# Transposed projection blocks in halves of 256 columns, with the high and low parts of x^T as one moving operand of 512

## The chip, the cores and the metric

The kernel runs on one core of a Trainium2 chip. Times are device microseconds of one launch. TensorE multiplies (a matmul streams the columns of its moving operand past a stationary one of up to 128x128, loaded before), VectorE (DVE), ScalarE (ACT) and GpSimd (POOL) do the elementwise work, SyncE (SP) issues most transfers. Matmul results land in PSUM, in banks of 512 fp32 columns per partition.

## What is computed

Two layers of a decoder trunk for 256 tokens of width 2048. Each layer normalises x, projects it once, runs four groups of four heads in parallel, gates each and projects back onto the residual:

```python
h = rms_norm(x, norm_g)
p = split_columns(h @ w_in)            # 2048 x 7700
fox  = forgetting_attention(...) * silu(p["fox_g"])
diff = rms_norm(differential_attention(...)) * silu(p["diff_g"])
moba = moba_attention(...) * silu(p["moba_g"])   # rotary on a part of q and k
gla  = rms_norm(gla_chunked(...)) * silu(p["gla_g"])
x = x + concat([fox, diff, moba, gla]) @ w_out   # 2048 x 2048
```

After both layers comes one more RMS norm. Everything is fp32, so the kernel computes each large product in three parts: an operand is split into a high part (rounded to fp32r, TensorE's fast fp32 form) and a low part (the rest), and a·b becomes ah·bh + ah·bl + al·bh.

## The kernel before, in words

**Blocks and steps.** `_blocks` (L103) lists the projections of a layer in order as blocks of up to 512 columns of weights. A "rows" block makes a result with tokens on the partitions: x^T is stationary, the weights move (n up to 512 columns), for two halves of 128 tokens. A "cols" block makes the transposed result, with weight columns on the partitions: 128 weight columns are stationary and x^T moves, 256 tokens. Nine blocks of a layer are "cols": GLA's q and k together, FoX's q, k and gate, the q and k of the differential attention, and MoBA's q, k and gate. The contraction has 16 tiles of 128 (kt). `_steps` (L138) cuts a block into steps that each take 512 KB of weights: two kt of 512 columns or four of up to 264. The first two blocks of layer 0 (GLA's low-rank input with a part of its gate, 264 columns, four steps; GLA's q and k, eight steps) are interleaved by groups of four kt, since x^T arrives in four chunks: one row step, two column steps, four times.

**The main loop** (L1296) runs over the steps. Each turn first emits `prepare(i + 2)`: the high part of the weights of the step after next on ScalarE (`hi_of`), the low part on VectorE (`lo_of`, source minus high), and the load of a later step on SP's queue. In the first twelve steps, one turn in three also splits a chunk of x^T (`split_xt`): four high and four low pieces of 256 columns. There are three buffers for the split weights, so ScalarE's split waits until TensorE has finished the step before the current one. Then `settle` evacuates finished blocks out of PSUM if the row statistics they need are ready, `multiply` emits the step's matmuls, and `tick` lets each pending task (attention and GLA are written as generators) advance by one part. Emission order is each engine's execution order.

**The planner.** `Costed` (L171) adds up what VectorE and ScalarE were given, at 0.06 us + 1.05 ns and 0.22 us + 0.88 ns per element (L232). `give_time` (L1259) credits both with TensorE's columns / 2400 us, 2.56 us a step, up to 3 us ahead. `tick` stops when an engine is past its credit. Before a step whose input is not ready, tasks are forced without limit.

**PSUM.** The pool `mm` has two buffers of two banks, one per block in turn; `side` has two more for the tasks. A "cols" block fills 4 x 256 columns: four weight groups, each [128, 256].

**The row statistics** of layer 0 come from x^T itself (`first_rms`, L1164): ScalarE squares each chunk in place, VectorE adds chunks 1 and 2 to the first and folds (two adds each for the first and the last), TensorE sums over partitions, POOL takes the power, TensorE spreads the result (`spread_rms`, L439). Until they are there no block is evacuated, as the scale is applied on the way out: `columns` (L457) multiplies a "cols" result by the spread scale, `rotated` (L881) also shuffles partitions for the rotary part, `gla_qk` (L542) scales q and k.

The matmuls of a "cols" step (L1246) are 24: for two kt and four weight groups c

```python
o, cs = ps[:, c * SEQ:(c + 1) * SEQ], slice(c * P, (c + 1) * P)
matmul(o, hi[:, cs], lh[:, kt], first and c % 2 == 0, False)
matmul(o, hi[:, cs], ll[:, kt], False, False)
matmul(o, lo[:, cs], lh[:, kt], False, last and c % 2 == 1)
```

with `lh` and `ll` the high and low parts of x^T. All operations on VectorE and ScalarE go through `Costed` and show line 183, matmuls line 279, transposes line 283; groups are told apart by their tiles.

Of the kernel before, what the change touches and what calls it, by code (L numbers as in the profile page):

```python
# [13 lines left out]
F32 = mybir.dt.float32  # L14
F32R = mybir.dt.float32r
# [86 lines left out]

def _blocks():  # L103

    def block(w, l, c0, n, kind, groups=(0, 1, 2, 3)):
        kts = [g * 4 + i for g in groups for i in range(4)]
        return {"w": w, "l": l, "c0": c0, "n": n, "kind": kind, "kts": kts, "per": 4 if n * 4 <= STEP_W else 2}

    out = []
    for l in range(DEPTH):  # L110
        for kind, c0, n in (
            ("rows", COL["gla_a"], 264),
            ("cols", COL["gla_q"], 512),
            ("rows", COL["gla_g"] + 248, 264),
            ("rows", COL["gla_v"], 512),
            ("rows", COL["fox_v"] + 258, 258),
            ("cols", COL["fox_q"], 512),
            ("cols", COL["fox_k"], 512),
            ("rows", COL["fox_v"], 258),
            ("cols", COL["fox_g"], 512),  # L120
            ("cols", COL["diff_q"], 512),
            ("cols", COL["diff_k"], 512),
            ("rows", COL["diff_g"], 512),
            ("rows", COL["diff_v"], 512),
            ("cols", COL["moba_q"], 512),
            ("cols", COL["moba_k"], 512),
            ("cols", COL["moba_g"], 512),
            ("rows", COL["moba_v"], 512),
        ):
            out.append(block("w_in", l, c0, n, kind))  # L130
        for chunk in range(4):
            cut = l + 1 == DEPTH and chunk == 3
            out.append(block("w_out", l, chunk * 512, 256 if cut else 512, "rows", (3, 0, 1, 2)))
    out.append(block("w_out", DEPTH - 1, D - 256, 256, "apart", (3, 0, 1, 2)))
    return out

# [76 lines left out]
def hybrid_trunk(  # L213
# [114 lines left out]

    def constants():

        nc.scalar.dma_start(ct, const[:, :KEPT])
        yield from until(("h", 0, 3))
        nc.scalar.dma_start(wa[0:16], gla_wa2.rearrange("l r e -> r l e"))
        nc.scalar.dma_start(wa[16:17].rearrange("p l e -> p (l e)"), gla_ba.rearrange("(o l) e -> o (l e)", o=1))
        yield
        s = []
        for name in ("sets", "upto", "masks"):
            c, n = CAT[name]
            s.append(s4.get([P, n], BF16))
            nc.scalar.dma_start(s[-1], const_b[:, c:c + n])  # L340
        yield
        c, n = CAT["neg"]
        nc.scalar.dma_start(neg_b, const_b[:, c:c + n])
        nc.scalar.dma_start(gng.rearrange("p l d -> p (l d)"), bcast_rows(gla_norm_g, 0, DEPTH * HD))
        nc.scalar.dma_start(fb.rearrange("p l h -> p (l h)"), bcast_rows(fox_fb, 0, DEPTH * H))
        yield
        lamt = s2.get([P, DEPTH, 4, 64])
        nc.scalar.dma_start(lamt.rearrange("p l a d -> p (l a d)"), bcast_rows(diff_lam, 0, DEPTH * 256))
        nc.scalar.dma_start(dng.rearrange("p l d -> p (l d)"), bcast_rows(diff_norm_g, 0, DEPTH * HD))
        yield  # L350
        v_.tensor_copy(a_r, s[0])
        v_.tensor_copy(upto_r, s[1])
        v_.tensor_copy(masks.rearrange("p l t -> p (l t)"), s[2])
        v_.tensor_scalar(ones_r, ident, 0.0, 1.0, op0=OP.mult, op1=OP.add)
        s4.put(*s)
        ready.add("constants")
        yield
        lp = s2.get([P, DEPTH, 2, 64])
        for l in range(DEPTH):
            v_.tensor_mul(lp[:, l], lamt[:, l, 0:4:2], lamt[:, l, 1:4:2])  # L360
            v_.tensor_reduce(ls2[:, l], lp[:, l], axis=AX.X, op=OP.add)
        s2.put(lp, lamt)
        yield
        a_.activation(ls2, ls2, AF.Exp)
        yield
        for l in range(DEPTH):
            li = 0.8 - 0.6 * math.exp(-0.3 * l)
            v_.scalar_tensor_tensor(lam[:, l:l + 1], ls2[:, l, 0:1], li, ls2[:, l, 1:2], op0=OP.add, op1=OP.subtract)
            v_.tensor_scalar(dng[:, l], dng[:, l], 1.0 - li, None, op0=OP.mult)

    hT = [big.tile([P, KT, SEQ], F32R, name="hTh"), big.tile([P, KT, SEQ], F32R, name="hTl")]
    mT = [big.tile([P, KT, SEQ], F32R, name="mTh"), big.tile([P, KT, SEQ], F32R, name="mTl")]


# [79 lines left out]
    def over(rb, n):  # L454
        return rb[:, None, :].to_broadcast([P, n, SEQ])

    def columns(l, ps, store):  # L457

        store = store.get([P, H, SEQ])
        v_.tensor_mul(store, ps, over(env["rb", l], H))  # L460
        return store

    def rows_of(l, ps, dst, eng):
        r = env["r", l]
# [74 lines left out]
            a_.activation(sg[:, m, :248], ps[m][:, 16:], AF.Silu, scale=r[:, m:m + 1])  # L539
        tasks.append(gla(l, an))  # L540

    def gla_qk(l, pqk):  # L542
        rb = env["rb", l]
        qkT = s4.get([P, 4, SEQ])
        v_.scalar_tensor_tensor(qkT[:, 0:2], pqk[:, 0:2], 0.125, over(rb, 2), op0=OP.mult, op1=OP.mult)
        v_.tensor_mul(qkT[:, 2:4], pqk[:, 2:4], over(rb, 2))
        env["gla_qk", l] = qkT
        ready.add(("gla_qk", l))

    def gla_gate(l, ps):  # L550
        r, sg = env["r", l], env["gla_sg", l]
# [224 lines left out]
        yield from split_group(l, gi, mixed, lambda: s4.put(mixed))  # L776

    def gate_columns(name):
        def done(l, ps):
            sgT = columns(l, ps, sgs)  # L780
            env[name, l] = sgT

            def silu():
                yield
                a_.activation(sgT, sgT, AF.Silu)
                ready.add((name, l))

            tasks.append(silu())

        return done  # L790
# [61 lines left out]
            yield  # L852
        ready.add(("forget", l))

    def fox_q(l, ps):
        env["fox_q", l] = columns(l, ps, s4)

    def fox_k(l, ps):
        kT = columns(l, ps, s4)

        def run():
            yield from until(("forget", l))
            yield
            yield from attend_columns(l, 0, "fox", env["fox_q", l], kT, env["forget", l])

        tasks.append(run())
# [14 lines left out]
    def rotated(name, table, half, last):  # L881
        swap = [i ^ half if i < 2 * half else i for i in range(32)]

        def done(l, ps):
            f = env[table, l]
            t = s4.get([P, H, SEQ])
            sw = s4.get([P, H, SEQ])
            v_.stream_shuffle(sw, ps, swap)
            v_.tensor_mul(t, ps, over(f[:, 0], H))

            def run():
                yield
                g_.tensor_mul(sw, sw, over(f[:, 1], H))
                yield
                yield
                v_.tensor_add(t, t, sw)
                s4.put(sw)
                if last:
                    s2.put(f)
                env[name, l] = t  # L900
                ready.add((name, l))

            tasks.append(run())

        return done

    def preceded(task, done):

        def both(l, ps):
            done(l, ps)  # L910
            tasks.append(task(l))

        return both

# [116 lines left out]
        yield from attend_columns(l, 2, "moba", env["moba_q", l], env["moba_k", l])  # L1031

    def started(task, done):
        def both(l, ps):
            tasks.append(task(l))
            done(l, ps)

        return both

# [55 lines left out]
    for l in range(DEPTH):  # L1095
# [10 lines left out]
            residual(0), residual(1), residual(2), residual(3),  # L1106
        )]
    dones.append((DEPTH - 1, None))
    blocks = []
    for z, (l, f) in zip(_BLOCKS, dones, strict=True):  # L1110
        own = {COL["diff_q"]: ("rope_d",), COL["moba_q"]: ("rope_m",)}.get(z["c0"] if z["w"] == "w_in" else None, ())
        blocks.append({"kind": z["kind"], "lhs": hT if z["w"] == "w_in" else mT, "n": z["n"], "per": z["per"],
                       "done": f and partial(f, l), "keys": {("r", l), ("rb", l)} | {(k, l) for k in own},
                       "need": "h" if z["w"] == "w_in" else "m", "l": l})
    plan = []
    for z in _steps():
# [11 lines left out]

    def load(i):
        s = plan[i]  # L1130
        if i < 12 and i % 3 == 0:
            load_x(i // 3)
        per, n = s["block"]["per"], s["block"]["n"]
        raw = wst.tile([P, STEP_W], F32, name="raw", bufs=RAW_BUFS)
        raw = raw[:, :per * n]
# [72 lines left out]
    def multiply(s):  # L1208
# [28 lines left out]
        for j, kt in enumerate(s["kts"]):  # L1237
# [6 lines left out]
                    matmul(o, lh[:, kt, ts], lo, False, False)  # L1244
                    matmul(o, ll[:, kt, ts], hi, False, last)
            else:  # L1246
                for c in range(4):
                    o, cs = ps[:, c * SEQ:(c + 1) * SEQ], slice(c * P, (c + 1) * P)
                    matmul(o, hi[:, cs], lh[:, kt], first and c % 2 == 0, False)
                    matmul(o, hi[:, cs], ll[:, kt], False, False)  # L1250
                    matmul(o, lo[:, cs], lh[:, kt], False, last and c % 2 == 1)

    def results(b):
        ps, n = b["ps"], b["n"]
        if b["kind"] == "rows":
            return ps[:, 0:n], ps[:, 512:512 + n]
        return ps.rearrange("p (c t) -> p c t", c=4)

    def give_time():  # L1259

# [5 lines left out]
    ahead = PART_BUFS - 1  # L1266

    def prepare(i):
        if 0 < i < 12 and i % 3 == 0:
            split_xt([i // 3 * 4 + k for k in range(4)])  # L1270
        if i < len(plan):
            parts_of(plan[i])
        if i + RAW_BUFS < len(plan):
# [12 lines left out]

    for i in range(RAW_BUFS):
        load(i)
    for i in range(ahead):
        prepare(i)  # L1290
    s4.put(zeros)
# [51 lines left out]
```

## Time and profile before

| | |
|---|---|
| median of 3 timed runs | 971.2 us (971.17 to 971.44) |
| the profiled execution: its time / its span | 971.15 / 969.3 us |
| granted clock of TensorE, mean | 0.998 of full |
| TensorE matmuls, weight loads | 6582 each, busy 954.8 and 877.9 us |
| VectorE / ScalarE / POOL busy | 587.7 / 463.3 / 64.3 us |
| transfers | 170.3 MB, mean 176 GB/s |

Matmuls overlap in the pipeline, so that a group's busy time and mean say little of what an instruction costs: a 256-column matmul shows some 280 ns and is followed by the next after some 120. The chain of work that ended last, and starts in the timeline, show that spacing.

### The profile page before, as it was taken

The page shows a single profiled execution, that of the slowest core. Times are in us where ns is not written, and L with a number is a line of the kernel's source. Part 1 is how long each engine was busy: PE and PEld are TensorE (multiplying, and loading weights), DVE is VectorE, ACT ScalarE, POOL GpSimd, SP SyncE. Part 2 cuts the span into 40 slices and gives each one's busy share as a digit, 9 for nine tenths or more (in the row PEclk, how much of TensorE's full clock was granted, in tenths as well). Part 3 has the DMA queues.
Part 4 walks back from the last instruction along what each step waited for, and adds up shares of the span by engine and source line. Part 5 has one row for each costly group of instructions (what it writes and reads, how often), then busy time and mean ns, then how long its engine had stood idle before and what let it go on. Part 6 is the DMA issues. An engine that isn't in the chain of part 4 may idle for free.

```text
span 969.3 us, 15989 instructions
## 1 busy us (share of the span) xinstructions
PE 954.8 (98%) x6582; PEld 877.9 (91%) x6582; DVE 587.7 (61%) x768; ACT 463.3 (48%) x617; POOL 64.3 (7%) x45
## 2 busy tenths in 40 slices
PE   9999999999999999999999999999999999999996
PEld 7989999999879998888899899999998899987886
DVE  7656766556755766455555667655664748655554
ACT  7564534343474336444446544345336543463442
POOL 0010200000010200000000102100011002100000
PEclk9999999999999999999999999999999999999999
DMA  8756554445555465555555544545555545645552
GB/s 300 216 184 203 176 191 150 156 158 184 175 177 181 137 199 167 161 182 177 186 172 164 161 151 157 174 161 164 163 174 174 186 158 180 227 161 166 189 184 105
DMA packets 49083, 170.32 MB, mean 176 GB/s; under 512 B 5969, under 2 KB 6513, under 8 KB 49010
## 3 DMA queue, kind: packets, MB, share of 16 engines
q1 hardware_dynamic: 46592, 165.24, 52.3%
q0 software_dynamic: 640, 2.10, 0.9%
q10 hardware_dynamic: 1778, 1.97, 0.7%
q8 instruction: 51, 0.84, 0.3%
q14 instruction: 22, 0.18, 0.1%
HBM read 167.19 MB, written 2.10 MB: 175 GB/s over the span
## 4 chain that ended last, share of the span: by engine, by line
PE 93%; ACT 3%; issue 1%; DVE 1%; DMA 1%; SPq 0%; POOLq 0%; POOL 0%; DVEq 0%; ACTq 0%
PE mm L279 84%; PE side L279 7%; PE side L283 2%; ACT hi L183 1%; ACT L183 1%; DVE lo L183 1%; DMA raw<-in_weights 1%; ACT four L183 0%; ACT gate L183 0%; DVE mTl L183 0%; DVE xs L183 0%; ACT two L183 0%; SPq L1127 0%; POOLq L1339 0%; POOL rf L381 0%
## 5 line engine op out<-in xcount | busy, mean ns | idle before, releaser
L183 DVE TENSOR_TENSOR lo<-raw,hi 128x1024 fp32r<-128x1024 f32 (+3 forms) x301 | 377.1, 1257 | 345.5 <-ACT hi L183 342.4
L183 ACT ACTIVATE hi<-raw 128x1024 fp32r<-128x1024 f32 (+3 forms) x301 | 318.0, 1059 | 469.6 <-PE mm L279 434.1
L279 PE MATMUL mm<-hTh,hi 128*128 128x256 f32 x1152 | 327.7, 284 | 0.0
L279 PE MATMUL mm<-hTh,lo 128*128 128x256 f32 x1152 | 324.5, 282 | 0.8 <-DVE lo L183 0.8
L279 PE MATMUL mm<-hTl,hi 128*128 128x256 f32 x1152 | 324.2, 281 | 0.0
L279 PEld LDWEIGHTS mm<-hTh,hi 128*128 128x128 f32 x1152 | 217.9, 189 | 1.0 <-issue 0.3
L279 PEld LDWEIGHTS mm<-hTh,lo 128*128 128x128 f32 x1152 | 217.6, 189 | 1.0 <-DVE lo L183 1.0
L279 PEld LDWEIGHTS mm<-hTl,hi 128*128 128x128 f32 x1152 | 217.3, 189 | 0.1
L279 PE MATMUL mm<-hi,hTh 128*128 128x512 f32 (+2 forms) x512 | 174.8, 343 | 0.4 <-ACT hi L183 0.2
L279 PE MATMUL mm<-lo,hTh 128*128 128x512 f32 (+2 forms) x512 | 172.4, 339 | 1.8 <-DVE lo L183 1.7
L279 PE MATMUL mm<-hi,hTl 128*128 128x512 f32 (+2 forms) x512 | 172.3, 338 | 0.0
L279 PEld LDWEIGHTS mm<-hi,hTh 128*128 128x128 f32 x512 | 95.9, 188 | 13.4 <-ACT hi L183 1.5
L279 PEld LDWEIGHTS mm<-lo,hTh 128*128 128x128 f32 x512 | 96.1, 188 | 13.3 <-DVE lo L183 3.1
L279 PEld LDWEIGHTS mm<-hi,hTl 128*128 128x128 f32 x512 | 95.9, 188 | 11.4
L279 PE MATMUL mm<-hi,mTh 128*128 128x512 f32 (+1 forms) x256 | 97.9, 382 | 0.0
L279 PE MATMUL mm<-hi,mTl 128*128 128x512 f32 (+1 forms) x256 | 97.1, 379 | 0.7 <-DVE mTl L183 0.7
L279 PE MATMUL mm<-lo,mTh 128*128 128x512 f32 (+1 forms) x256 | 97.0, 379 | 0.0
L279 PEld LDWEIGHTS mm<-hi,mTl 128*128 128x128 f32 x256 | 48.1, 188 | 11.5 <-DVE mTl L183 1.6
L279 PEld LDWEIGHTS mm<-hi,mTh 128*128 128x128 f32 x256 | 48.1, 188 | 9.4
L279 PEld LDWEIGHTS mm<-lo,mTh 128*128 128x128 f32 x256 | 48.1, 188 | 9.3
L279 PE MATMUL side<-four,four 128*128 128x128 f32 (+2 forms) x288 | 38.0, 288 | 0.0
L183 ACT ACT_TABLE_LOAD x27 | 34.6, 1283 | 0.5
(155 smaller groups left out, 626.5 us busy)
## 6 DMA issues: line engine op xcount, KB each, us to landing
raw<-in_weights SPq DMA_DIRECT2D x272, 512.0 KB, 3.5
raw<-in_weights SPq DMA_DIRECT2D x16, 516.0 KB, 3.5
raw<-in_weights SPq DMA_DIRECT2D x15, 528.0 KB, 3.5
xs<-in_x SPq DMA_DIRECT2D x4, 512.0 KB, 4.6
four<-in_xt SPq DMA_DIRECT2D x3, 512.0 KB, 7.4
out<-xs SPq DMA_DIRECT2D x6, 256.0 KB, 3.4
two<-in_const POOLq DMA_DIRECT2D x4, 256.0 KB, 3.6
two<-in_final_norm_g POOLq DMA_DIRECT2D x4, 256.0 KB, 5.9
```

The source lines that it names most:

```text
L183: return f(*args, **kw)
L279: t_.matmul(out, lhsT, rhs, start=start, stop=stop)
L283: t_.transpose(out, src, ident)
```

## The change

The "cols" blocks of 512 weight columns become two blocks of 256, `half` 0 and 1; each has four steps of four kt in place of eight steps of two, so a step has the same bytes and the same columns. The high and low parts of x^T are kept side by side in one tile, `hTp`, and one matmul of 512 moving columns multiplies the high weights by both, into a whole bank; a second one of 256 columns adds the low weights times the high part into the bank's first half. On the way out `summed` copies the bank's second half on ScalarE and adds the first on VectorE; the scaling follows from there. Users of a block get their slots at half 0 and start their tasks at half 0 or 1. The interleaved start has eight steps in place of twelve, one x chunk for two of them. The load of the constants is issued at the start, behind the first four weight loads in program order, on ScalarE's queue. The descriptor space of POOL's transfers is set to 4096 bytes.

```diff
+    def block(w, l, c0, n, kind, groups=(0, 1, 2, 3), half=None):
...
+            if kind == "cols":
+                out += [block("w_in", l, c0 + half * 256, 256, kind, half=half) for half in range(2)]
+            else:
+                out.append(block("w_in", l, c0, n, kind))
...
     def constants():
 
-        nc.scalar.dma_start(ct, const[:, :KEPT])
         yield from until(("h", 0, 3))
...
-    hT = [big.tile([P, KT, SEQ], F32R, name="hTh"), big.tile([P, KT, SEQ], F32R, name="hTl")]
+    hTp = big.tile([P, KT, 2, SEQ], F32R, name="hTp")
+    hT = [hTp[:, :, 0], hTp[:, :, 1]]
...
-    def columns(l, ps, store):
-
-        store = store.get([P, H, SEQ])
-        v_.tensor_mul(store, ps, over(env["rb", l], H))
-        return store
+    def summed(ps):
+
+        t = wk.tile([P, 2, SEQ], F32, name="both", tag="both", bufs=2)
+        a_.activation(t, ps[:, :, 1], AF.Copy)
+        v_.tensor_add(t, ps[:, :, 0], t)
+        return t
+
+    def columns(l, ps, store, half):
+
+        v_.tensor_mul(store[:, half * 2:half * 2 + 2], summed(ps), over(env["rb", l], 2))
...
+    def gla_qk(l, ps, half):
+        rb = over(env["rb", l], 2)
+        if half == 0:
+            env["gla_qk", l] = s4.get([P, 4, SEQ])
+            v_.scalar_tensor_tensor(env["gla_qk", l][:, 0:2], summed(ps), 0.125, rb, op0=OP.mult, op1=OP.mult)
+        else:
+            v_.tensor_mul(env["gla_qk", l][:, 2:4], summed(ps), rb)
+            ready.add(("gla_qk", l))
...
-        def done(l, ps):
+        def done(l, ps, half):
             f = env[table, l]
-            t = s4.get([P, H, SEQ])
-            sw = s4.get([P, H, SEQ])
-            v_.stream_shuffle(sw, ps, swap)
-            v_.tensor_mul(t, ps, over(f[:, 0], H))
+            if half == 0:
+                env["turn", l] = [s4.get([P, H, SEQ]), s4.get([P, H, SEQ])]
+            t, sw = env["turn", l]
+            hs = slice(half * 2, half * 2 + 2)
+            z = summed(ps)
+            v_.stream_shuffle(sw[:, hs], z, swap)
+            v_.tensor_mul(t[:, hs], z, over(f[:, 0], 2))
+            if half == 0:
+                return
...
     def load(i):
         s = plan[i]
-        if i < 12 and i % 3 == 0:
-            load_x(i // 3)
+        if i < 8 and i % 2 == 0:
+            load_x(i // 2)
...
-                for c in range(4):
-                    o, cs = ps[:, c * SEQ:(c + 1) * SEQ], slice(c * P, (c + 1) * P)
-                    matmul(o, hi[:, cs], lh[:, kt], first and c % 2 == 0, False)
-                    matmul(o, hi[:, cs], ll[:, kt], False, False)
-                    matmul(o, lo[:, cs], lh[:, kt], False, last and c % 2 == 1)
+                for c in range(2):
+                    o, cs = ps[:, c * 512:(c + 1) * 512], slice(c * P, (c + 1) * P)
+                    matmul(o, hi[:, cs], hTp[:, kt].rearrange("p z t -> p (z t)"), first, False)
+                    matmul(o[:, :SEQ], lo[:, cs], lh[:, kt], False, last)
...
     def prepare(i):
-        if 0 < i < 12 and i % 3 == 0:
-            split_xt([i // 3 * 4 + k for k in range(4)])
+        if 0 < i < 8 and i % 2 == 0:
+            split_xt([i // 2 * 4 + k for k in range(4)])
...
     for i in range(RAW_BUFS):
         load(i)
+    nc.scalar.dma_start(ct, const[:, :KEPT])
     for i in range(ahead):
         prepare(i)
...
-    nc = bacc.Bacc("TRN2", target_bir_lowering=False, num_devices=1)
+    nc = bacc.Bacc("TRN2", target_bir_lowering=False, num_devices=1, dynamic_dma_scratch_size=4096)
```

## Rows read from the trace of the kernel before

**Rows 1.** The page: busy times by engine, and the chain that ended last, by engine.

```profile
PE 954.8 (98%) x6582; PEld 877.9 (91%) x6582; DVE 587.7 (61%) x768; ACT 463.3 (48%) x617; POOL 64.3 (7%) x45
...
PE 93%; ACT 3%; issue 1%; DVE 1%; DMA 1%; SPq 0%; POOLq 0%; POOL 0%; DVEq 0%; ACTq 0%
```

**Rows 2.** Stretches: start:end and length; busy us per engine, clock, DMA share, GB/s.

```profile
core 0: us, PE busy (x) PEld busy (x) DVE busy (x) ACT busy (x) POOL busy (x), PEclk, DMA share, GB/s
111.00:135.00 24.00, 24.00 (x204) 23.75 (x204) 21.87 (x47) 8.34 (x9) 4.18 (x4) 1.00 0.61 204
172.80:189.80 17.00, 17.00 (x145) 17.00 (x145) 10.16 (x11) 7.13 (x14) 0.00 (x0) 1.00 0.42 144
423.00:445.00 22.00, 22.00 (x96) 17.81 (x96) 12.66 (x14) 10.32 (x16) 0.00 (x0) 1.00 0.58 188
9.00:12.00 3.00, 2.24 (x17) 1.88 (x16) 1.83 (x2) 3.00 (x5) 0.00 (x0) 1.00 1.04 414
10.80:34.00 23.20, 23.20 (x195) 23.20 (x195) 19.98 (x27) 16.96 (x25) 0.00 (x0) 1.00 0.83 274
```

**Rows 3.** TensorE's waits: total us, how many, the longest.

```profile
PE mm L279 <- DVE lo L183: 2.4, 4, 0.8
...
PEld mm L279 <- DVE lo L183: 4.0, 5, 1.1
```

**Rows 4.** The chain of waits in order of time: start, us, what.

```profile
2.59 5.79 DMA raw<-in_weights
...
33.79 0.79 PE side L279 x8
...
37.69 0.68 PE side L279 x4
...
172.78 17.10 PE mm L279 x144
...
423.00 22.22 PE mm L279 x96
...
955.52 0.43 DVE xs L183
```

**Rows 5.** Groups by shape: one of the three of 1152 matmuls.

```profile
L279 PE MATMUL mm<-hTh,hi 128*128 128x256 f32 x1152 | 327.7, 284 | 0.0
```

**Rows 6.** Groups by shape: ways out of PSUM; busy us, mean ns.

```profile
L183 DVE TENSOR_TENSOR xs<-mm,xs 128x512 f32<-128x512 f32 x14 | 9.0, 683 | 0.0
...
L183 ACT ACTIVATE four<-mm,rstd 128x512 f32<-128x512 f32 x12 | 7.5, 676 | 0.0
...
L183 DVE TENSOR_TENSOR four<-mm,rb 128x1024 f32<-128x1024 f32 x4 | 4.9, 1217 | 0.0
```

**Rows 7.** Timeline of VectorE in the start: start us, length, instruction.

```profile
9.51 1.23 DVE L183 TENSOR_TENSOR lo<-raw,hi 128x1024 fp32r<-128x1024 f32 x1 [0.97 <-ACT hi L183]
...
12.54 1.67 DVE L183 SCALAR_TENSOR_TENSOR hTl<-four,ngt,hTh 128x256 fp32r<-128x256 f32 x4
14.12 1.25 DVE L183 TENSOR_TENSOR lo<-raw,hi 128x1056 fp32r<-128x1056 f32 x1
15.33 1.23 DVE L183 TENSOR_TENSOR four<-four,four 128x1024 f32<-128x1024 f32 x1
...
30.41 1.14 DVE L183 TENSOR_TENSOR four<-four 128x512 f32<-128x512 f32 x2
```

**Rows 8.** Timeline of ScalarE: the first evacuation of layer 0.

```profile
37.63 1.08 ACT L183 ACTIVATE hi<-raw 128x1056 fp32r<-128x1056 f32 x1 [2.87 <-PE mm L279]
38.73 1.28 ACT L183 ACT_TABLE_LOAD   x1
...
40.96 0.47 ACT L183 ACTIVATE gate<-mm,rstd 128x248 f32<-128x248 f32 x1 [0.30 <-DVE an L183]
```

**Rows 9.** Timeline of TensorE: two waits, near the end of layer 0 and early in layer 1.

```profile
411.20 0.50 PE L279 MATMUL mm<-hi,mTl 128*128 128x512 f32 x1 [0.36 <-DVE mTl L183]
...
511.46 0.28 PE L283 MATMUL side<-ct,an 128*16 128x128 f32 x1 [0.24 <-DVE an L183]
```

**Rows 10.** The page's issues of transfers: KB each, us to landing.

```profile
ct<-in_const ACTq DMA_DIRECT2D x1, 129.0 KB, 3.8
```

More of the change, by code (lines that the diff above doesn't have):

```diff
@@ L103, in _blocks @@
 def _blocks():
-    def block(w, l, c0, n, kind, groups=(0, 1, 2, 3)):
+    def block(w, l, c0, n, kind, groups=(0, 1, 2, 3), half=None):
         kts = [g * 4 + i for g in groups for i in range(4)]
-        return {"w": w, "l": l, "c0": c0, "n": n, "kind": kind, "kts": kts, "per": 4 if n * 4 <= STEP_W else 2}
+        return {"w": w, "l": l, "c0": c0, "n": n, "kind": kind, "kts": kts, "per": 4 if n * 4 <= STEP_W else 2, "half": half}
     out = []
@@ L129, in _blocks @@
         ):
-            out.append(block("w_in", l, c0, n, kind))
+            if kind == "cols":
+                out += [block("w_in", l, c0 + half * 256, 256, kind, half=half) for half in range(2)]
+            else:
+                out.append(block("w_in", l, c0, n, kind))
         for chunk in range(4):
@@ L540, in gla_first @@
         tasks.append(gla(l, an))
[L542 to L548, printed above, removed]
+    def gla_qk(l, ps, half):
[6 more added lines that the diff above has]
+            ready.add(("gla_qk", l))
     def gla_gate(l, ps):
@@ L778, in gate_columns @@
     def gate_columns(name):
-        def done(l, ps):
-            sgT = columns(l, ps, sgs)
-            env[name, l] = sgT
+        def done(l, ps, half):
+            if half == 0:
+                env[name, l] = sgs.get([P, H, SEQ])
+            sgT = env[name, l]
+            columns(l, ps, sgT, half)
+            if half == 0:
+                return
             def silu():
@@ L853, in fox_forget, with fox_q, fox_k @@
         ready.add(("forget", l))
[L855 to L859, printed above, removed]
+    def fox_q(l, ps, half):
+        if half == 0:
+            env["fox_q", l] = s4.get([P, H, SEQ])
+        columns(l, ps, env["fox_q", l], half)
+    def fox_k(l, ps, half):
+        if half == 0:
+            env["fox_k", l] = s4.get([P, H, SEQ])
+        kT = env["fox_k", l]
+        columns(l, ps, kT, half)
+        if half == 0:
+            return
         def run():
@@ L882, in rotated, with done @@
         swap = [i ^ half if i < 2 * half else i for i in range(32)]
-        def done(l, ps):
+        def done(l, ps, half):
             f = env[table, l]
-            t = s4.get([P, H, SEQ])
-            sw = s4.get([P, H, SEQ])
-            v_.stream_shuffle(sw, ps, swap)
-            v_.tensor_mul(t, ps, over(f[:, 0], H))
+            if half == 0:
+                env["turn", l] = [s4.get([P, H, SEQ]), s4.get([P, H, SEQ])]
[4 more added lines that the diff above has]
+            v_.tensor_mul(t[:, hs], z, over(f[:, 0], 2))
+            if half == 0:
+                return
             def run():
@@ L907, in preceded, with both @@
     def preceded(task, done):
-        def both(l, ps):
-            done(l, ps)
-            tasks.append(task(l))
+        def both(l, ps, half=None):
+            done(l, *([ps] if half is None else [ps, half]))
+            if half != 1:
+                tasks.append(task(l))
         return both
@@ L1033, in started, with both @@
     def started(task, done):
-        def both(l, ps):
-            tasks.append(task(l))
-            done(l, ps)
+        def both(l, ps, half):
+            if half == 0:
+                tasks.append(task(l))
+            done(l, ps, half)
         return both
@@ L1108, in hybrid_trunk @@
     dones.append((DEPTH - 1, None))
+    dones = iter(dones)
     blocks = []
-    for z, (l, f) in zip(_BLOCKS, dones, strict=True):
+    for z in _BLOCKS:
+        if z["half"] != 1:
+            l, f = next(dones)
         own = {COL["diff_q"]: ("rope_d",), COL["moba_q"]: ("rope_m",)}.get(z["c0"] if z["w"] == "w_in" else None, ())
         blocks.append({"kind": z["kind"], "lhs": hT if z["w"] == "w_in" else mT, "n": z["n"], "per": z["per"],
-                       "done": f and partial(f, l), "keys": {("r", l), ("rb", l)} | {(k, l) for k in own},
+                       "done": f and (partial(f, l) if z["half"] is None else partial(f, l, half=z["half"])), "keys": {("r", l), ("rb", l)} | {(k, l) for k in own},
                        "need": "h" if z["w"] == "w_in" else "m", "l": l})
@@ L1256, in results @@
             return ps[:, 0:n], ps[:, 512:512 + n]
-        return ps.rearrange("p (c t) -> p c t", c=4)
+        return ps.rearrange("p (c z t) -> p c z t", c=2, z=2)
     def give_time():
```

## The prediction

> **What bounds the kernel now.** I read the page's busy table and its chain first. TensorE is busy 98% of the span and carries 93% of the chain [rows 1], so the question is how fast it issues and where it waits. The stretches come next: in 22 us of row blocks and in 17 us of column blocks TensorE is busy throughout at clock 1.00, its upper level of 2.4 GHz, while VectorE has about 60% [rows 2]. TensorE's waits are last: the longest entry on the matmul row is 2.4 us over four waits, and its weight loads waited 4.0 us in all for VectorE's low halves [rows 3]. So almost nothing is hidden behind other engines. The time is the count of matmuls times their spacing, plus a start until the second weight step is split, plus the tail after 955.5 us [rows 4], which the change leaves alone.
>
> Spacing, not the modelled length of a matmul, is the price. A column stretch issues 144 matmuls of 256 columns in 17.10 us: 118.8 ns each. A row stretch issues 96 of 512 in 22.22 us: 231.5 ns [rows 4]. Two short ones cost 237.6, one long one 231.5: 6.1 ns go with an instruction saved.
>
> **The change part by part, against the profiled run's own 971.15 us** (span 969.3 and 1.85 around it; the median of the timed runs is 971.2).
>
> *The matmuls.* 3 x 1152 matmuls of 256 columns [rows 5] become 1152 of 512 and 1152 of 256: 1152 pairs that cost 237.6 now cost 231.5. 1152 x 6.1 ns = **7.0 us less**. The columns are the same, and the 1152 weight loads that go with them already run beside matmuls, so no more than that is on offer from the spacing rows: 6.1 ns is all that they show as fixed per instruction. The Trainium skill (TensorE: Matmul & The Clock Gate, section "Wait — 56ns, not 53.3ns?") gives about 2.5 ns fixed per matmul at the upper clock; by it the sum would have 2.9 us in place of 7.0. The measured rows decide for the sum.
>
> *Leaving PSUM.* A whole block left by one VectorE multiply of 1024 (1217 ns). Now each of two halves takes a ScalarE copy of 512 (like 676 ns), a VectorE add of 512 out of PSUM (like 683) and a multiply of 512 out of SBUF (taken as the same 683) [rows 6]: VectorE 2 x 1.37 = 2.73 for 1.22, so 1.5 us more a block, 27 us over 18 blocks; ScalarE 2 x 0.68, 24 us. Rotated blocks pay the same extra add. Cover: a step lasts 2.8 us, VectorE's split of the next weights takes 1.23 of it [rows 7], and the splits run two steps ahead. In the quiet column stretch VectorE has 6.8 us of 17 free [rows 2]: zero there. The thin place is 111 to 135 us, where GLA's work fills 21.9 of 24 us of VectorE [rows 2] and 1.5 us more eat most of the 2.1 left; if the cover goes, the low half comes late by 0 to 1 us, in each layer. I take 0.3 for both layers, near the lower end, because that stretch has no idle TensorE now.
>
> A half block is 4 steps, 11 us, and there are two PSUM buffers, so a buffer must be empty 11 us after its block ended, not 22. An evacuation queued behind one split and one copy is out in about 4 us: zero, but for the two places below.
>
> *The start, VectorE.* Before, twelve steps (one GLA row step, two column steps, four times) cover the splitting of four x chunks; now eight do. Work per chunk is unchanged, so it stands against less TensorE time. From the end of the second step's low half (10.7 us) to the folded squares of the last chunk, VectorE has three chunk splits of 1.67, five weight splits of 1.23 to 1.25, two adds of 1.23 and two folds of 1.14 [rows 7]: 5.0 + 6.2 + 2.5 + 2.3 = 16.0 us. Some 0.09 overlaps at each of eleven joins, 1.0 us; about as much is lost to ScalarE, which has a square, four high halves of x and a weight split to do before the third step's low half can start. So 16 stands. TensorE in that time has the rest of step 1, two row steps of 264 columns and two column half steps: 2.6 + 2 x 2.9 + 2 x 2.8 = 14.0 us (24 matmuls of 264 columns at 122 ns, between the two spacings; 2.8 is eight pairs at 350.3). The sums over the squares (x8 at 33.79 [rows 4]) are issued on TensorE right behind, so it waits the difference, some of it already on the splits before: 2.0 us, and I take **2.2** for the joins that don't fit. Ends: 0, if the folds find room; 4.8, if adds and folds come on top as a whole. Today VectorE has 20.0 busy of the 23.2 us [rows 2], which places it near the middle.
>
> *The start, the first buffer.* The third block now begins at step 8, in the buffer of the first, whose evacuation waits for the row statistics. ScalarE does one weight split, a table load and two gates from 37.63 to 41.43, 3.8 us, all after the step that ended when it began [rows 8]; TensorE has one half step and the 0.68 us spread of the statistics [rows 4], 3.3 to 3.5. **0.5 us** of wait, between 0 and 1.5. In layer 1 the same block order gives the same race; TensorE already waits 0.24 there for the same evacuation [rows 9], so **0.3 more**.
>
> *The queues.* The constants' 129 KB [rows 10] move from behind the start on ScalarE's queue to its front, ahead of the wait that opens the chain (a weight transfer, 5.79 us [rows 4]). The DMA engines are full then, 414 GB/s [rows 2]: 129 KB is 0.3 us, ahead of the second weights. I take **0.3**; ends 0 and 0.35. The issue itself falls where ScalarE waits for its first weights. On SP the second x chunk passes the third weights, the same 512 KB: it lands about one transfer (1.3 us by that rate) sooner, and the third weights, needed next, that much later, which falls inside ScalarE's square and high halves of x: 0, or 1.3 us without them. Slot requests of the rotated blocks come 11 us sooner; no task waits for them on the path I can see: 0. The smaller descriptor space touches only POOL's eight transfers, each due tens of us later: 0.
>
> Sum: -7.0 + 0.3 + 2.2 + 0.5 + 0.3 + 0.3 = -3.4: **967.8 us**.
>
> **The rivals.** (a) *Start fully hidden.* If the folds slip, only the queue's 0.3 remains: 964.5. For: TensorE is gapless there now. Against: 16 us of VectorE work in 14. (b) *Weight loads set the pace.* If a 256-column matmul is paced by its load and not its columns, the one left behind a 512-column matmul runs at half of 231.5, 115.8: another 1152 x 3.0 = 3.5 us, 964.3. For: one load per matmul, busy 91% of the span [rows 1]. Against: a load not hidden would show in both spacings alike, and 6.1 ns is all that is common. The Trainium skill (the same page, section "LDWEIGHTS (loading the stationary operand)") puts a load of 128 columns at P/1.2, an estimate of 107 ns, close to what a short matmul lasts; no run here shows a load by itself. (c) *The start eats the gain.* Adds and folds exposed whole, 4.8 for 2.2, and the buffer's 1.5 for 0.5: 967.8 + 3.6 = 971.4. For: every engine's queue is in order, so one late split delays all behind it. (d) *Slower: a slipped step before the output projection.* MoBA's last group arrives 0.36 us late as it is [rows 9]. Its tasks advance one part per step, and only while the planner's credit for VectorE and ScalarE is not used up. The point is one skipped turn: the rest, forced, then queues behind the next weight split: 1.1 us on ScalarE [rows 8], 1.23 on VectorE, and the group's own low half of the same size, 3.5 us, of which 0.4 is paid today: 3.1 a layer, 967.8 + 6.2 = 974.0. Against: by the planner's own prices (L232) a step with an evacuation costs VectorE 1.14 + 2 x 0.60 = 2.3 of the 2.56 us it is credited. (e) *The change doesn't shorten the matmuls.* The 231.5 comes from weights moving, not x; if x and its low half cost 237.6, no gain, 971.15 + 3.6 = 974.8. Against: operands of one type, side by side. The Trainium skill's 2.5 ns (page and section above) would land between, at 971.9.
>
> **How the numbers follow.** About 0.2%, 1.9 us, is what a measurement of this kernel tells from no change: faster is under 969.3. Chances: forecast 0.55, with its own range 965.5 to 969.6 from the ends of the start's terms; (a) 0.10; (b) 0.05; (c) 0.17; (d) 0.08; (e) 0.05. Faster: nearly all of the forecast, (a), (b) and a little of (c): 0.67. Slower: (d), (e) and a little of (c): 0.14. The rest, 0.19, within 0.2%. The range leaves out (d) and (e): 963.9 to 971.9.
>
> **What would show it.** Right: matmul rows of 1152 at 512 columns with two 256-column groups gone, a column half step of four k tiles at 2.80 us where 24 short ones take 2.85; a TensorE wait of some 2 us near 26 to 28 us ahead of the sums of squares; a short one at step 8 behind the gates; ScalarE and VectorE busier by 24 and 27 us with no new waits after 60 us. Wrong: a half step that is not shorter than 2.85, or much shorter; TensorE gapless until 34 us; a wait of 3 us before the group of 411 us.

## The result and the profile after

The changed kernel takes 964.89 us (964.84 to 964.92), the kernel before 971.18 beside it: a ratio of 0.9936 (95% interval 0.9919 to 0.9953), 6.3 us less. The profiled execution took 964.92 us with a span of 963.1.

The page of the changed kernel: busy times, the chain by engine, and the groups of the column blocks and of the new way out of PSUM.

```profile
PE 946.3 (98%) x5430; PEld 819.5 (85%) x5430; DVE 616.9 (64%) x836; ACT 480.2 (50%) x653; POOL 68.3 (7%) x45
...
PE 91%; ACT 4%; DVE 2%; issue 2%; DMA 1%; SPq 0%; POOLq 0%; POOL 0%; DVEq 0%; ACTq 0%
...
L282 PE MATMUL mm<-hTp,hi 128*128 128x512 f32 x1152 | 407.3, 396 | 0.8 <-ACT gate L186 0.8
L282 PE MATMUL mm<-hTp,lo 128*128 128x256 f32 x1152 | 323.9, 281 | 0.8 <-DVE lo L186 0.8
...
L186 DVE TENSOR_TENSOR both<-mm,both 128x512 f32<-128x512 f32 x36 | 24.6, 684 | 0.0
L186 ACT ACTIVATE both<-mm 128x512 f32<-128x512 f32 x36 | 20.9, 580 | 0.0
```

Against [rows 1], 1152 matmuls and as many weight loads are gone, and TensorE is as full as before. VectorE has 29 us more and ScalarE 17; ScalarE's copy took 580 ns where 676 was taken. Of [rows 5] one group of 512 columns and one of 256 are left.

The chain of the changed kernel, the stretches that answer to [rows 4]: start, us, what.

```profile
2.59 5.77 DMA raw<-in_weights
...
173.71 16.74 PE mm L282 x96
...
421.13 22.16 PE mm L282 x96
```

The row stretch is as before within 0.06 us: 22.16 us for 96. The column stretch has 48 pairs (one long matmul and one short) in 16.74 us, **348.8 ns a pair**; before, three short ones took 356.3 (17.10 us for 48 times three). So the new kernel is ahead by 7.5 ns for each of 1152 pairs, 8.6 us in all, where the forecast had 6.1 ns and 7.0 us.

TensorE's timeline in the changed kernel: its waits in the start from the second step's low half on, the first matmul of the block after the start, and three later waits.

```profile
10.75 0.38 PE L282 MATMUL mm<-hTp,lo 128*128 128x256 f32 x1 [0.77 <-DVE lo L186]
14.31 0.39 PE L282 MATMUL mm<-lo,hTp 128*128 128x264 f32 x1 [0.59 <-DVE lo L186]
26.80 0.80 PE L282 MATMUL side<-one,four 128*128 128x1 f32 x6 [0.80 <-DVE four L186]
34.44 0.51 PE L282 MATMUL mm<-hTp,hi 128*128 128x512 f32 x1 [0.58 <-ACT gate L186]
...
45.73 0.28 PE L282 MATMUL mm<-hi,hTp 128*128 128x264 f32 x1
...
409.36 0.50 PE L282 MATMUL mm<-hi,mTl 128*128 128x512 f32 x1 [0.36 <-DVE mTl L186]
509.33 0.28 PE L286 MATMUL side<-ct,an 128*16 128x128 f32 x1 [0.29 <-DVE an L186]
509.83 0.50 PE L282 MATMUL mm<-hTp,hi 128*128 128x512 f32 x1 [0.22 <-ACT gate L186]
```

The first was there before (0.76 us at 10.79). The next three are new: for VectorE's low half at the third step, for the folded squares, and for the gates that hold the first PSUM buffer. Counted from start to start, with the restart, they are 0.76, 0.85 and 0.73 us. The block after the start (GLA's second gate part) begins at 45.73 us. In the kernel before it began at 43.89:

```profile
43.89 0.28 PE L279 MATMUL mm<-hi,hTh 128*128 128x264 f32 x1
```

That is 1.84 later, although its predecessors' 64 pairs save 0.5 us: the start lost 2.3 us. In the changed kernel the way out of the last output block begins at 949.69 us; before, by the chain of [rows 4], at 955.52:

```profile
949.69 0.42 DVE L186 TENSOR_TENSOR xs<-mm,xs 128x256 f32<-128x256 f32 x1 [3.18 <-PE mm L282]
```

So between the start and there the changed kernel wins 7.7 us, and another 0.3 in the transfers at the end.

VectorE in the start of the changed kernel, from the second step's low half to the folds of the last chunk.

```profile
9.47 1.23 DVE L186 TENSOR_TENSOR lo<-raw,hi 128x1024 fp32r<-128x1024 f32 x1 [0.95 <-ACT hi L186]
10.82 1.69 DVE L186 SCALAR_TENSOR_TENSOR hTp<-four,ngt,hTp 128x256 fp32r<-128x256 f32 x4
12.99 1.26 DVE L186 TENSOR_TENSOR lo<-raw,hi 128x1056 fp32r<-128x1056 f32 x1 [0.49 <-ACT hi L186]
...
25.50 1.15 DVE L186 TENSOR_TENSOR four<-four 128x512 f32<-128x512 f32 x2
```

From 10.70 to 26.65 it is 15.95 us with a single gap of 0.49, against the 16 of the forecast. The gap is a wait for ScalarE, and it lies just ahead of the low half that TensorE waits for at 14.31: that first new wait is in large part ScalarE's. Behind it VectorE works without a gap until the folds are done, and the second is VectorE's alone.

### The profile page after: what moved, and what is told of

The parts are those of the page before. It is cut to its first block, busy times and chain, and to the rows that moved or that the text cites. A ratio compares the mean times of both kernels' runs of the same rounds, so it can differ in the third digit from the quotient of the medians.

```text
span 963.1 us, 13772 instructions
## 1 busy us (share of the span) xinstructions
PE 946.3 (98%) x5430; PEld 819.5 (85%) x5430; DVE 616.9 (64%) x836; ACT 480.2 (50%) x653; POOL 68.3 (7%) x45
## 4 chain that ended last, share of the span: by engine, by line
PE 91%; ACT 4%; DVE 2%; issue 2%; DMA 1%; SPq 0%; POOLq 0%; POOL 0%; DVEq 0%; ACTq 0%
PE mm L282 82%; PE side L282 7%; PE side L286 2%; ACT hi L186 1%; DVE lo L186 1%; ACT L186 1%; ACT four L186 1%; DMA raw<-in_weights 1%; ACT gate L186 1%; DVE mTl L186 0%; DVE four L186 0%; DVE hTp L186 0%; DVE xs L186 0%; ACT two L186 0%; ACT hTp L186 0%
## 5 line engine op out<-in xcount | busy, mean ns | idle before, releaser
L282 PE MATMUL mm<-hTp,hi 128*128 128x512 f32 x1152 | 407.3, 396 | 0.8 <-ACT gate L186 0.8
L282 PE MATMUL mm<-hTp,lo 128*128 128x256 f32 x1152 | 323.9, 281 | 0.8 <-DVE lo L186 0.8
L282 PE MATMUL mm<-hi,hTp 128*128 128x512 f32 (+2 forms) x1024 | 261.0, 341 | 0.9 <-DVE hTp L186 0.4
L282 PEld LDWEIGHTS mm<-hTp,hi 128*128 128x128 f32 x1152 | 216.5, 188 | 49.6 <-ACT gate L186 1.3
L282 PEld LDWEIGHTS mm<-hTp,lo 128*128 128x128 f32 x1152 | 216.7, 188 | 1.2 <-DVE lo L186 1.1
L282 PEld LDWEIGHTS mm<-hi,hTp 128*128 128x128 f32 x1024 | 176.1, 188 | 25.7 <-ACT hi L186 2.4
L282 PE MATMUL mm<-lo,hTp 128*128 128x512 f32 (+2 forms) x512 | 172.5, 339 | 2.4 <-DVE lo L186 2.3
L282 PEld LDWEIGHTS mm<-lo,hTp 128*128 128x128 f32 x512 | 96.0, 188 | 14.0 <-DVE lo L186 3.9
L282 PEld LDWEIGHTS side<-four,four 128*128 128x128 f32 (+1 forms) x288 | 31.2, 190 | 2.7 <-issue 0.7
L186 DVE TENSOR_TENSOR both<-mm,both 128x512 f32<-128x512 f32 x36 | 24.6, 684 | 0.0
```

The lines of the kernel that those rows point to most:

```text
L186: return f(*args, **kw)
L282: t_.matmul(out, lhsT, rhs, start=start, stop=stop)
```

## Experiments

All edits are against the changed kernel. Times are medians with ratios to the kernel before on the same chip (971.36 us for e_split, e_group, e_twelve and e_buf, 971.12 for the others). The intervals reach about 1.2 us to either side for most of the runs, mainly because single runs of the kernel before spread from 970.38 to 972.51 us. Ratios alone therefore don't show differences of 2 us or less between two changed kernels; where one is claimed below, the runs of the two kernels don't overlap and the trace shows the place.

**e_split**: the merged matmul is taken apart again, nothing else.

```diff
-                    matmul(o, hi[:, cs], hTp[:, kt].rearrange("p z t -> p (z t)"), first, False)
+                    matmul(o[:, :SEQ], hi[:, cs], lh[:, kt], first, False)
+                    matmul(o[:, SEQ:], hi[:, cs], ll[:, kt], False, False)
```

> Everything of the changed kernel stays (half blocks, start, evacuation); only the 512-column matmul is issued as two of 256 again, so each unit of weight group and k tile has three short matmuls. Theory 'a fixed price per instruction, 6.1 ns, as the stretches of before give': 1152 x 6.1 = 7.0 us above the changed kernel's 964.9, 971.9. Theory 'a short matmul behind a long one of other weights is also quicker than one among short ones' (pairs at 348.8 ns in the changed trace, three short ones at 356.4): 1152 x 7.6 = 8.7 us more, 973.6. The start's waits, if they stay the same, make this the changed kernel's cost without its gain.

Measured 973.68 us, ratio 1.0023 (1.0014 to 1.0032): 8.8 us above the changed kernel (8.6 when each is taken against the kernel before on its chip), the second theory's number, and slower than the kernel before. The same stretch of the chain has the spacing of before:

```profile
174.64 17.10 PE mm L282 x144
```

So the merge is the whole gain, and the rest of the change costs 2.3 us net.

**e_group**: the same matmuls, two long ones and then two short ones.

```diff
                     matmul(o, hi[:, cs], hTp[:, kt].rearrange("p z t -> p (z t)"), first, False)
+                for c in range(2):
+                    o, cs = ps[:, c * 512:(c + 1) * 512], slice(c * P, (c + 1) * P)
                     matmul(o[:, :SEQ], lo[:, cs], lh[:, kt], False, last)
```

> The same matmuls in another order: for a k tile the two long ones, then the two short ones, so that half of the short ones follow a short one and half of the long ones a long one. Theory 'each length has its own spacing, whatever stands before it': 348.8 ns per pair as now, 964.9 within 0.3. Theory 'a short one is cheap only behind a long one, since its weights are loaded in the longer time': half the pairs go back to 231.5 + 118.8, so +0.7 ns on average or up to +1.5 per pair: 0.8 to 1.7 us more, 965.7 to 966.6.

Measured 966.80 us, ratio 0.9952 (0.9940 to 0.9965): 1.9 us more with the same instructions. The chain:

```profile
173.47 16.83 PE mm L282 x96
```

350.6 ns a pair is close to the sum that the forecast read from [rows 4], 231.5 + 118.8 = 350.3. The second theory's place was right, and its range fell short by 0.2 us. The price of a matmul depends on its neighbour; alternation is worth 1.9 ns a pair in this stretch.

**e_cross**: lengths alternate, but, except in a block's first k tile, the short one behind a long one belongs to the other bank and weight group.

```diff
-                for c in range(2):
-                    o, cs = ps[:, c * 512:(c + 1) * 512], slice(c * P, (c + 1) * P)
-                    matmul(o, hi[:, cs], hTp[:, kt].rearrange("p z t -> p (z t)"), first, False)
-                    matmul(o[:, :SEQ], lo[:, cs], lh[:, kt], False, last)
+                o = [ps[:, c * 512:(c + 1) * 512] for c in range(2)]
+                xt2 = hTp[:, kt].rearrange("p z t -> p (z t)")
+                for a, b2 in ((0, 0), (1, 1)) if first else ((0, 1), (1, 0)):
+                    matmul(o[a], hi[:, a * P:(a + 1) * P], xt2, first, last and a == 1)
+                    matmul(o[b2][:, :SEQ], lo[:, b2 * P:(b2 + 1) * P], lh[:, kt], False, last and b2 == 0)
```

> The long and the short matmuls alternate as in the changed kernel, but but for a block's first k tile the short one behind a long one goes to the other bank and the other weight group (long 0, short 1, long 1, short 0). The grouped order cost 350.6 ns a pair, the alternating one 348.8. Theory 'what counts is that lengths alternate, so that each load runs beside a matmul of another length': 348.8, 964.9 within 0.4. Rival 'what counts is that a pair stays in one bank, or streams the same x twice in a row': half of the pairs' seams are lost, up to the grouped order's 966.8.

Measured 964.90 us, ratio 0.9934 (0.9922 to 0.9947), and in the chain

```profile
173.62 16.75 PE mm L282 x96
```

It is the alternation that counts, not that a long matmul and the short one behind it share bank and weight group. This run alone leaves a rival: both alternating orders change the bank at every second matmul, the grouped one at every matmul. e_split answers it. It changes the bank after every third matmul, the kernel before after every sixth, and both take 17.10 us for 144: a change of bank has no price that shows. In all three orders the long matmul has the high weights and the short one the low weights, so that lengths and weight parts aren't told apart.

The Trainium skill (TensorE: Matmul & The Clock Gate, section "Back-to-back issue gap") says that in a stream of loads and matmuls the spacing is set by both together. Three orders of the same instructions at 348.8, 348.9 and 350.6 ns don't contradict it; that it is the load's time beside each matmul which makes the difference is not shown here, as no run shows a load without its matmul.

**e_twelve**: three blocks share the start again, twelve steps, the third in a side buffer.

```diff
-            key = ((j + per - 1) // 4, i) if i < 2 else (9, i)
+            key = ((j + per - 1) // 4, i) if i < 3 else (9, i)
...
-        if i < 8 and i % 2 == 0:
-            load_x(i // 2)
+        if i < 12 and i % 3 == 0:
+            load_x(i // 3)
...
-        if 0 < i < 8 and i % 2 == 0:
-            split_xt([i // 2 * 4 + k for k in range(4)])
+        if 0 < i < 12 and i % 3 == 0:
+            split_xt([i // 3 * 4 + k for k in range(4)])
...
-            b["ps"] = mm.tile([P, 1024], F32, name="mm")
+            third = b is blocks[2]
+            b["ps"] = side.get([P, 1024]) if third else mm.tile([P, 1024], F32, name="mm")
...
             b["done"](results(b))
+            if b is blocks[2]:
+                side.put(b["ps"])
```

> The start gets its twelve steps back: both halves of GLA's q and k are interleaved with the first row block, one row step and two column steps per x chunk, the second half in a buffer of the side pool. Theory 'eight steps of TensorE work don't cover VectorE's share of four x chunks, and the first buffer is needed before it is out': the three waits of the start (0.76 and 0.85 us for VectorE, 0.73 us for the gates) go, 964.9 - 2.3 = 962.6. Rival 'the start is bound by its transfers or by ScalarE': the waits stay where they are in time, 964.9, or move to the second chunk.

Measured 962.34 us, ratio 0.9907 (0.9893 to 0.9920): 2.5 us less than the changed kernel for 2.3 expected. TensorE's waits (total us, how many, the longest), first in the changed kernel:

```profile
PE mm L282 <- DVE lo L186: 3.0, 5, 0.8
...
PE side L282 <- DVE four L186: 0.8, 1, 0.8
PE mm L282 <- ACT gate L186: 0.8, 2, 0.6
```

Here the folds' entry is gone, and most of the gates':

```profile
PE mm L282 <- DVE lo L186: 2.4, 4, 0.8
...
PE side L286 <- DVE an L186: 0.3, 1, 0.3
...
PE mm L282 <- ACT gate L186: 0.2, 1, 0.2
```

The low halves' 2.4 us is the figure of [rows 3]. The gates' 0.2 is layer 1, where the blocks stand as in the changed kernel. The edit restores the twelve steps and gives the third block a buffer of its own, both at once; that the gates' wait is one for the buffer is e_buf's to show.

**e_buf**: the first block leaves PSUM by VectorE alone.

```diff
             v_.tensor_scalar(an[:, m], ps[m][:, 0:16], r[:, m:m + 1], None, op0=OP.mult)
-            a_.activation(sg[:, m, :248], ps[m][:, 16:], AF.Silu, scale=r[:, m:m + 1])
+            v_.tensor_scalar(sg[:, m, :248], ps[m][:, 16:], r[:, m:m + 1], None, op0=OP.mult)
+        for m in range(2):
+            a_.activation(sg[:, m, :248], sg[:, m, :248], AF.Silu)
```

> The first block of a layer leaves PSUM by VectorE alone (two multiplies of 248 columns more), and ScalarE's silu then reads SBUF, behind its table load. Theory 'the third block waits for the first one's buffer, held by ScalarE's split, table load and gates': the wait of 0.73 us at 33.6 goes, and 0.3 to 0.5 in layer 1: 963.7 to 964.0. Rival 'what waits is the chain of the row statistics itself': nothing moves, 964.9.

Measured 964.38 us, ratio 0.9927 (0.9915 to 0.9939): 0.5 us less, half of what was expected. The ratio doesn't tell it from the changed kernel; the trace shows the same 0.5 us, 0.27 at the third block in layer 0 and 0.20 more in layer 1, where the wait for `an` (0.29) is gone. The wait for the gates has another name, and is clearly shorter in layer 0 alone:

```profile
34.17 0.47 PE L282 MATMUL mm<-hTp,hi 128*128 128x512 f32 x1 [0.30 <-DVE gate L186]
...
509.36 0.47 PE L282 MATMUL mm<-hTp,hi 128*128 128x512 f32 x1 [0.20 <-DVE gate L186]
```

The buffer is what is waited for. Taking ScalarE out of its release gives back part; VectorE's copies stand behind its own split of weights, and that split behind ScalarE's.

**e_double**: every evacuation doubled on both engines, unseen by the planner.

```diff
+        z = wk.tile([P, 2, SEQ], F32, name="again", tag="again", bufs=1)
+        nc.scalar.activation(t, ps[:, :, 1], AF.Copy)
         a_.activation(t, ps[:, :, 1], AF.Copy)
+        nc.vector.tensor_copy(z, ps[:, :, 0])
         v_.tensor_add(t, ps[:, :, 0], t)
```

> Each evacuation of a half block is doubled on both engines: ScalarE copies the bank's second half twice, VectorE copies the first half once more to a tile that nobody reads; the planner isn't told of the additions. 36 x 0.58 = 21 us more on ScalarE, 36 x 0.68 = 25 us more on VectorE. Theory 'evacuation is hidden behind TensorE, as no wait after the start grew': 964.9 to 965.4, new waits if any in 111 to 135 us and its twin in layer 1. Rival 'the added work of the change is partly exposed in the dense stretches (0.3 us forecast)': 0.3 to 2 us more, 965.2 to 967.

Measured 966.63 us, ratio 0.9951 (0.9937 to 0.9965): 1.7 us more for 46 us of added work. That is the rival's number, not the theory's. It isn't in the stretch that the forecast named, since every block up to 291 us begins 0.1 us late as the first does. The chain of this run from 330 us on shows where it begins:

```profile
332.53 4.96 PE mm L282 x27
337.50 1.14 DVE lo L186
```

In the rotary blocks of MoBA, where VectorE also finishes the differential group, a low half comes late: 0.6 us, once in each layer. The rest is a later arrival of MoBA's last group, 0.64 us of wait for 0.36, and its like. With one evacuation the low half's row is absent and MoBA's wait is the 0.36 of before, so the added work is covered as it is, but doubling would not be.

**e_ct**: the constants' load behind the first two steps.

```diff
-    nc.scalar.dma_start(ct, const[:, :KEPT])
     for i in range(ahead):
         prepare(i)
+    nc.scalar.dma_start(ct, const[:, :KEPT])
```

> The constants' load is issued behind the first two steps' splits on ScalarE's queue, some 8 us later, in place of its front. Forecast's term '129 KB ahead of the second weights cost 0.3 us': 964.6. Theory 'the second weights land between 8.0 and 8.85 us after the start from run to run, in runs with the load in front, and at 8.4 without: no cost that can be told': 964.9 within 0.3.

Measured 964.72 us, ratio 0.9934 (0.9921 to 0.9946), with runs from 964.40 to 965.24: no cost that these runs can tell from none. ScalarE's first split of the second weights, which opens the chain, starts at 7.88 us here, 8.38 in the changed kernel and, with the same load in front, 8.00 in e_group and 8.85 in e_twelve:

```profile
7.88 1.06 ACT L186 ACTIVATE hi<-raw 128x1024 fp32r<-128x1024 f32 x1 [1.13 <-DMA raw<-in_weights]
```

With the load in front, the landing moves by 0.85 us between executions, more than the term. Such a shift goes through to the total: this execution starts the third block at 33.94 us, 0.50 ahead of the changed kernel's, and is 0.52 us shorter (964.40 for 964.92).

**e_best**: e_twelve and e_buf together.

> The twelve-step start and the first block's way out by VectorE together. Theory: 962.3 of the twelve-step start, less what is left of the buffer's wait in layer 1 (0.2 to 0.5 us; in layer 0 the third block no longer needs that buffer): 961.8 to 962.1. Rival 'VectorE's added 0.9 us in layer 0 delays its splits there': 962.3 or more.

Measured 962.04 us, ratio 0.9906 (0.9892 to 0.9919): 2.9 us faster than the changed kernel and 9.1 than the one before. That is in the theory's range, but what e_buf adds to e_twelve, 0.3 us, is less than the intervals, and the runs of the two overlap.

## Why the prediction was right, and where its terms were off

It said faster, 967.8 in a range of 963.9 to 971.9; 964.9 lies inside, 2.9 us below the number and 0.6 below the forecast's own narrower range. So the direction and the kinds of waits were right by working, while the place in the range owes something to luck: it is the part kept for the rivals (a) and (b), and neither of them happened. Term by term:

| term | forecast | measured | by |
|---|---|---|---|
| matmuls | -7.0 | -8.6 | 7.5 ns a pair in the chain; e_split, 8.6 to 8.8 |
| start, VectorE | +2.2 | +1.6 | timeline: 0.76 and 0.85; part of the first is ScalarE's |
| start, first buffer | +0.5 | +0.7 | timeline; e_buf |
| the same in layer 1 | +0.3 | about +0.3 | 0.29 and 0.22 of wait for 0.24 |
| constants in front | +0.3 | none told apart | e_ct |
| dense stretch | +0.3 | 0 | TensorE busy 24.00 of 24 us in 111 to 135; e_double |
| last transfers | 0 | -0.3 | one trace of each kernel; not tried |

**The mis-sized term** is the first: "1152 pairs that cost 237.6 now cost 231.5". Both prices are right where they were read, among matmuls of one length, and the grouped order pays about their sum (350.6 for 350.3). The step that failed is to carry them into a stream in which lengths alternate. The bound drawn from it, "no more than that is on offer from the spacing rows", was too tight: 7.5 ns, not 6.1, went with an instruction. The 2.5 ns of the Trainium skill (the same page, section "Wait — 56ns, not 53.3ns?"), which by an estimate would have left 2.9 us, is further off, and the measurement decides.

**The start** went by its mechanism, in the places named: a wait for the split, one ahead of the sums of squares at 26 us, one behind the gates at step 8. In place of the one wait of some 2 us near 26 us there were two, the first of them at 14 us and mostly behind ScalarE. The 2.2 was the forecast's 2.0 and a guess "for the joins that don't fit"; they fit, as VectorE's 15.95 us show, and TensorE had more of its own to do: from 10.75 to 26.80 us less the two waits it is 14.4 us, where 14.0 was counted. That e_twelve takes all of it back shows that the eight-step start, with its third block in the first one's buffer, is the cause.

**The queues.** "129 KB is 0.3 us, ahead of the second weights" treated the load as one more link before a known arrival; the arrival itself is less certain than that.

**The rivals.** (a) gave 964.5 and (b) 964.3, and the measurement is beside both, but neither is what happened. The start was not hidden: it cost 2.3 us. Of (b)'s 3.0 ns a pair, 1.5 (against the sum from [rows 4]) to 1.9 (against e_group) exist, though that loads are their cause is open. Two rivals can agree with a total whose terms are others. (c) would have shown as waits of 6 us before 35 us; there are 2.3. (d) did not come: MoBA's last group waits 0.36 us as in [rows 9], and even e_double adds only 0.28 to it. (e) is refuted by e_split: without the merge the kernel is 8.6 to 8.8 us slower.

The earlier slot requests and the smaller descriptor space were not tried by themselves; no wait in the trace after is for either.

## What to carry to other kernels

When TensorE is full, count instructions: the same columns in fewer matmuls gained 0.9% here, and a spacing must be read in the mix of lengths that the new stream will have. Restaging a kernel's steady state also restages its start: here splitting was balanced against the matmuls of three steps per chunk, two per chunk no longer covered it, and the 2.3 us lost came back by interleaving a third block. Before an added cost is called hidden, double it: the place where it comes out tells which stretch is the thin one.

## What was not expected of the hardware

The same matmuls with the same operands cost 350.6 ns a pair in the order long, long, short, short and 348.8 alternating, whether the short one behind a long one writes the same bank or the other; the grouped order made the total 1.9 us longer. And a 512 KB transfer at the start, in the same place of its queue, was ready between 8.00 and 8.85 us after the start from one execution to another, in eight profiles of kernels whose changes lie behind it.
